# Output projection by seven products: other homes for the weight pieces, x added by accumulating transfers, another place for later loads

## The chip, the cores and the metric

The kernel runs on one core of a Trainium2 chip, in float32 accuracy throughout. The metric is the device time of one execution in microseconds (us), the median of the runs shown. A profile is one more execution, taken by the hardware profiler. In its rows PE is the matrix engine, PEld its weight loads, DVE, ACT and POOL the vector, scalar and GpSimd engines, SP the engine that issues most loads; SPq and POOLq are the queues of DMAs that SP and POOL issue. L955 is line 955 of the kernel.

## The reference

One decoder layer on x of 512 tokens by 1024 columns: a normalised input projection, two parallel token mixers, a gated merge, an output projection with a gated residual add, a second norm and a gated MLP of 2816 hidden columns.

```python
merged = (jax.nn.sigmoid(ga) * (out_a @ w_branch_swa[l])
          + jax.nn.sigmoid(gd) * (out_d @ w_branch_diff[l]))
x = x + gate1 * (merged @ w_out[l])

h2 = _rmsnorm(x, norm2_g[l]) * (1.0 + scale2) + shift2
x = x + gate2 * _conv_ffn(h2, w_up[l], conv_w[l], conv_b[l], w_down[l])
...
return _rmsnorm(x, final_g)
```

The change lies in `x + gate1 * (merged @ w_out)`, a product of 512x1024 by 1024x1024, and in what is loaded meanwhile for `h2 @ w_up`.

## The kernel before

**Seven products.** The output projection cuts merged and w_out (the gate is multiplied into its columns first) into two by two quarters and computes the product by seven quarter products in place of eight, named m1, m5, m6, p2, p3, m7, p4 in the order in which PE runs them (`mul_out`, L1178 is the matmul). Each has 512x512 weights, cut into two pieces p = 0, 1 of 256 rows, held as 128x1024 numbers. Every operand is split into a high part, rounded to the fast matmul format by a cast on ACT, and a low part, the rest, taken by a subtraction on DVE (`split`, L120); each product is then three matmuls: high by high, high by low, low by high. A product is 24 matmuls of 128x512, 12 for each piece.

**The chain of weights.** The weights of m1, m5 (called t1), m6 (t2) and p4 (t4) are running sums. Piece p of them lives in one buffer, `chain_o[p]` (chain_oy for p = 0, chain_ofgb for p = 1), which starts as a quarter of w_out. When the piece in it has been split, a DMA with accumulation, issued by POOL (`add_by_dma`, L955), adds the next term: first a quarter kept in DRAM scratch (b12g0, b12g1), then p3raw0 or p3raw1 (the piece of p3's weights), then p2raw0 or p2raw1. p3raw itself gets b12g added when p3's piece (b22) has been split, and then is the piece of m7 (t3). So each accumulating transfer waits for a split, and the cast of the next piece waits for the transfer.

**Homes.** A split piece (its two parts, whi and wlo) is kept either in a ring of three (`ring_home`, wp, WB = 3), where it waits for the piece three before to have been used, or in a buffer of its own, gT2 (`own_home`). Before the change the pieces m1p0, t2p0, b22p0 and t4p0 take gT2 in turn, the others the ring. The buffers vvh and vvl (`gpart(0)` and `gpart(1)`) hold xn0 and xn1 all the while; xn1 and the second half of the g1b tile keep three product sums (c1, c3, c2).

**Sums.** PE accumulates in three pairs of banks: oU (m1, then m6 and m7 on top, then p4), oV (m5, then p3), oX (p2). x1 is a tile of 512x1024 into which SP loads x in four transfers of 512 KB (L1150). Where a sum is wanted before its bank goes on accumulating, `keep_sum` has ACT copy the pair to c1, c2 or c3, and POOL accumulates that copy into x1 from SBUF. At the end DVE subtracts or adds the banks into x1 directly (`merge_x`, L1257), ACT squares (`square2`, L1266) for the second norm, and a few small DVE steps make its factor (L1275, L1283, L165 to L167). p4 goes on in bank oU only after DVE has subtracted m7's sum (x1 rows 256 to 511, second half of the columns).

**What follows.** xn rows are transposed on PE into th, ACT and DVE scale them (L1303, L1301) to bh and bl, and the up stage (`mul_slot`, L1202) runs in slots J. Its weights come by SP (`load_raw`, L990: wa for a11 and a12, s1, s3, a22), the s1 and s3 blocks with a second block that POOL accumulates (L992). wa1_0 and wa1_1 are split ahead of their slot into early_outh and early_outl (`hi_early`, `lo_early`, L1344, L1348).

**The order.** From `man` on, PE, DVE, ACT and POOL run in the order in which the code is written (manual schedule); SP's order was left to the scheduler. The transfers that POOL issues form one queue, as do SP's. A wait blocks what stands behind it on its engine.

Of the kernel before, what the change touches and what calls it, by code (L numbers as in the profile page):

```python
# [9 lines left out]
F32R = mybir.dt.float32r  # L10
# [37 lines left out]
def kernel(  # L48
# [896 lines left out]
    chain_o = [bp.tile([P, 2, S], F32, tag=g, name=f"chain_o{g}") for g in ("y", "fgb")]  # L945
    g4 = gpart(4, [P, 2, D], "g1b")
    g1b, c2 = g4[:, 0], g4[:, 1].rearrange("p (u n) -> p u n", u=2)
    st = gpart(3, [P, 2, 4, 256], "s1_t1")
# [5 lines left out]
    def add_by_dma(dst, src):  # L954
        nc.gpsimd.dma_start(dst, src, accum_op=ALU.add)  # L955
# [192 lines left out]

    for t in range(NT):
        nc.sync.dma_start(x1[:, t], xd[t * P : (t + 1) * P, :])  # L1150

# [174 lines left out]
    man = ExitStack()  # L1326
    man.enter_context(tc.manual_schedule(engines={nc.vector.engine, nc.scalar.engine, nc.tensor.engine, nc.gpsimd.engine}))
# [48 lines left out]
    keep_sum(c2, oU, 0, 1, -1.0)
    piece("p3", 1, braw["p3", 1], ring_home("b22p1"))
    add_by_dma(braw["p3", 1], scratch_o(1))
    split_quarter(opA[0][:, 2], opA[1][:, 2], q11)
# [6 lines left out]
    mul_out("p3")
    piece("m7", 0, braw["p3", 0], ring_home("t3p0"))
    for u in range(2):
        merge_x(u, 0, oX[u], ALU.subtract)
    piece("m7", 1, braw["p3", 1], ring_home("t3p1"))  # L1390
    hi_early(2)
    lo_early(2)
    mul_out("m7")
    square2(0, 0)
    square2(1, 0)
    piece("p4", 0, chain_o[0], own_home("t4p0"))
    norm_first(0, 0)
# [3 lines left out]
    norm_start(0, 1)  # L1401
    piece("p4", 1, chain_o[1], ring_home("t4p1"))
# [536 lines left out]
```

## Time and profile before

| | |
|---|---|
| median of 3 runs | 703.98 us (703.77 to 705.58) |
| profiled execution, its own time | 704.4 us |
| its span | 702.6 us |
| mean granted PE clock | 0.981 |
| matmuls | 3997 |
| products m1 to m7 of the projection, and what runs beside them, to p4's first matmul | 292.73 to 351.55 |
| p4 and the second norm, to the unbroken part of the up stage | 351.55 to 393.85 |

Columns of a timeline: start, duration, engine, line, operation, out<-in by the program's names without numbers (t1p is piece 0 or 1 of t1; chain_ofgb<-b12g is the accumulating DMA of b12g1), shapes, count, and in brackets the engine's idle time before it and what ended it. The start of a DMA row is its issue. A table of windows has one row for each stretch: length, busy time of each engine with its instructions, granted clock, busy share of the 16 DMA engines, GB/s. In a DMA view "DMA to landing" is the time from issue to the last byte; q0 software_dynamic is what POOL issues, q1 hardware_dynamic what SP issues.

### The profile page before, as it was taken

Reading aid. Unit: us, or ns where it says so; the run is one execution under the profiler, and the core shown is the slowest. Engines: PE = TensorE matmul, PEld = TensorE weight load, DVE = VectorE, ACT = ScalarE, POOL = GpSimd, SP = SyncE. Lnnn points to the kernel's source line nnn. Section 1 sums busy time; section 2 is a strip of 40 time slices with the busy share of each in tenths; the row PEclk is TensorE's granted clock in tenths of the full one; section 3 lists DMA queues with packets and bytes.
Section 4 is the critical chain, followed back from the end, with each engine's and each line's share of the span. In section 5 each row is a group of like instructions: output and inputs, shape, how many; then the busy total and the mean of one; then the engine's idle time right before and its main releaser. Section 6 shows DMA issues by size and latency. Waiting matters only on the chain.

```text
span 702.6 us, 10831 instructions
## 1 busy us (share of the span) xinstructions
PE 674.0 (96%) x3997; PEld 594.3 (85%) x3997; DVE 575.6 (82%) x1028; ACT 413.5 (59%) x722; POOL 101.1 (14%) x125
## 2 busy tenths in 40 slices
PE   9999999999999999978598999999999999999995
PEld 8888888888888888756388999999999999888884
DVE  6988986967876677756556999988899999979997
ACT  7668876565653233246458666555656667655665
POOL 2000000011321100125000111111101101640300
PEclk9999999999999999988889999999999999999999
DMA  9951323434448976479942697887998758998903
GB/s 352 408 210 61 117 64 115 154 114 143 160 126 287 306 244 210 91 221 237 201 110 40 184 225 180 222 201 227 234 238 195 191 175 234 182 206 229 164 1 120
DMA packets 77061, 129.65 MB, mean 185 GB/s; under 512 B 4496, under 2 KB 49712, under 8 KB 77008
## 3 DMA queue, kind: packets, MB, share of 16 engines
q1 hardware_dynamic: 54272, 95.04, 39.8%
q0 software_dynamic: 22448, 33.71, 27.5%
q8 instruction: 31, 0.51, 0.3%
q10 hardware_dynamic: 288, 0.21, 0.1%
q14 instruction: 22, 0.18, 0.1%
HBM read 122.11 MB, written 3.16 MB: 178 GB/s over the span
## 4 chain that ended last, share of the span: by engine, by line
PE 35%; issue 9%; DVE 3%; DMA 2%; POOL 1%; ACT 1%; POOLq 0%; SPq 0%; DVEq 0%; ACTq 0%
PE up L1202 28%; PE dc L1868 6%; DMA s_t<-in_w_up_dram 1%; PE oU L1178 1%; DMA s<-in_w_up_dram 1%; POOL b L1854 1%; DVE p2wl L120 0%; DVE p_wlo L1024 0%; ACT sqo L1266 0%; DVE p2a L120 0%; DVE chain_kvB L1728 0%; DVE chain_outl L1730 0%; POOL s L992 0%; DVE p3wl L120 0%; DVE t4p_wlo L120 0%
## 5 line engine op out<-in xcount | busy, mean ns | idle before, releaser
L1202 PE MATMUL up<-bh,p_whi 128*128 128x256 f32 x232 | 65.8, 283 | 1.2 <-ACT p_whi L1020 1.2
L1202 PE MATMUL up<-bh,p_wlo 128*128 128x256 f32 x232 | 65.8, 283 | 0.8 <-DVE p_wlo L1024 0.8
L1202 PE MATMUL up<-bl,p_whi 128*128 128x256 f32 x232 | 65.7, 283 | 0.0
L992 POOL DMA_DIRECT2D s<-in_w_up_dram x21 | 29.0, 1504 | 181.1 <-DMA s<-in_w_up_dram 76.7
L1202 PEld LDWEIGHTS up<-bh,p_whi 128*128 128x128 f32 x232 | 44.5, 192 | 1.4 <-ACT p_whi L1020 1.4
L1202 PEld LDWEIGHTS up<-bh,p_wlo 128*128 128x128 f32 x232 | 44.5, 192 | 1.0 <-DVE p_wlo L1024 1.0
L1202 PEld LDWEIGHTS up<-bl,p_whi 128*128 128x128 f32 x232 | 44.5, 192 | 0.0
L1020 ACT CAST m_whi<-s 128x1024 fp32r<-128x1024 f32 x31 | 32.5, 1047 | 18.8 <-DVE s L1014 10.9
L1024 DVE TENSOR_TENSOR m_wlo<-s,m_whi 128x1024 fp32r<-128x1024 f32 x31 | 37.8, 1219 | 1.3 <-ACT m_whi L1020 1.3
L1202 PE MATMUL up<-t_kvB,m_whi 128*128 128x256 f32 x176 | 32.5, 284 | 0.2 <-DVE t_kvB L1324 0.2
L1202 PE MATMUL up<-t_outl,p_whi 128*128 128x256 f32 x176 | 32.2, 283 | 0.5 <-DVE pairs L1242 0.5
L1202 PE MATMUL up<-t_outh,m_whi 128*128 128x256 f32 x176 | 32.2, 283 | 0.0
L798 DVE CUSTOM_DVE_ANT_0 ra<-ra,csb 128x1024 f32<-128x1024 f32 x24 | 29.0, 1220 | 0.8 <-DMA ra<-in_w_ada_t_dram 0.7
L1202 PE MATMUL up<-t_kvA,m_whi 128*128 128x256 f32 x160 | 29.3, 283 | 0.0
L1202 PEld LDWEIGHTS up<-t_kvB,m_whi 128*128 128x128 f32 x176 | 27.5, 192 | 0.7 <-DVE t_kvB L1324 0.4
L1202 PEld LDWEIGHTS up<-t_outl,p_whi 128*128 128x128 f32 x176 | 27.4, 192 | 0.7 <-issue 0.7
L1202 PEld LDWEIGHTS up<-t_outh,m_whi 128*128 128x128 f32 x176 | 27.4, 192 | 0.0
L1020 ACT CAST p_whi<-wa 128x1024 fp32r<-128x1024 f32 x18 | 18.8, 1044 | 14.0 <-PE up L1202 8.6
L708 ACT ACTIVATE sd<-sd,dmx 128x128 f32<-128x128 f32 (+3 forms) x32 | 17.7, 556 | 14.9 <-DVE dmx L693 14.8
L1024 DVE TENSOR_TENSOR p_wlo<-wa,p_whi 128x1024 fp32r<-128x1024 f32 x18 | 22.0, 1223 | 4.0 <-ACT p_whi L1020 2.7
L1202 PE MATMUL up<-t_outh,m_wlo 128*128 128x256 f32 x88 | 25.0, 284 | 0.3 <-DVE m_wlo L1024 0.3
L1202 PEld LDWEIGHTS up<-t_kvA,m_whi 128*128 128x128 f32 x160 | 24.9, 192 | 0.0
(669 smaller groups left out, 2268.2 us busy)
## 6 DMA issues: line engine op xcount, KB each, us to landing
ra<-in_w_ada_t_dram SPq DMA_DIRECT2D x24, 512.0 KB, 4.1
wa<-in_w_up_dram SPq DMA_DIRECT2D x22, 512.0 KB, 5.5
s<-in_w_up_dram SPq DMA_DIRECT2D x21, 512.0 KB, 5.6
s<-in_w_up_dram POOLq DMA_DIRECT2D x21, 512.0 KB, 8.0
adaw<-in_w_ada_t_dram SPq DMA_DIRECT2D x15, 512.0 KB, 10.2
a<-in_w_up_dram SPq DMA_DIRECT2D x11, 512.0 KB, 5.0
b<-in_w_down_dram SPq DMA_DIRECT2D x10, 512.0 KB, 5.0
w<-in_w_first_dram SPq DMA_DIRECT2D x8, 512.0 KB, 10.2
```

Of the source, the lines that this page charges most:

```text
L708: nc.scalar.activation(pm[m], pm[m], AF.Exp, bias=mx[:, m : m + 1], scale=-1.0, accum_out=(l0, l1)[m])
L798: nc.vector.tensor_tensor_reduce(r, r, csb, 1.0, 0.0, ALU.mult, ALU.add, late_mod[:, idx : idx + 1])
L992: nc.gpsimd.dma_start(dst, upblock(*blk), accum_op=ALU.add)
L1020: nc.scalar.copy(W[J, name][0], R[J, SRC[name]])
L1024: nc.vector.tensor_sub(lo, R[J, SRC[name]], hi.bitcast(F32))
L1178: nc.tensor.matmul(o[u], a(k, u), w[:, q], start=name in ("m1", "m5", "p2") and k == 0 and x == 0, stop=k == 3 and x == 2, skip_group_chec ...
L1202: nc.tensor.matmul(o[u], w[:, k, cu], b[:, k], start=name in ("p1", "m5", "p2") and k == 0 and x == 0, stop=k == 3 and x == 2, skip_group_ ...
L1854: nc.gpsimd.dma_start(w, wblock(g, *add), accum_op=ALU.add)
L1868: nc.tensor.matmul((bank2[u] if o is None else o)[:, sl], a[:, q, cu], b[:, q, sl], start=first_mm and x == 0, stop=last_mm and x == 2, sk ...
```

## The change

Four things change in the projection's stage; the seven products, their order on PE and the numbers of casts and subtractions stay.

1. **Homes.** m1p0 goes to the ring and t1p0 to gT2; t2p0 and t3p0 go to vvh, t2p1 and t3p1 to vvl, b22p0 to gT2, t4p0 and t4p1 to the ring. xn0 and xn1 are taken after that. The copies c1, c2 and c3 are gone, and the g1b tile is half as large.
2. **x1.** ACT writes the first sum straight into x1 (`start_x`), and POOL accumulates x from DRAM on top of it, for three of the four blocks; only the fourth (rows 256 to 511, first 512 columns) is loaded by SP.
3. **Order of splits.** p2p0's split, opB's split, p3's pieces, opA's third part and m7's and p4's pieces are written earlier; the splits of wa1_0 and wa1_1 later (the second behind p4's first matmuls), and so is the subtraction of oX.
4. **SP in written order**, with s3 and s1 and a22 of slots 0 and 1 written ahead of p4.

```diff
-    piece("m1", 0, chain_o[0], own_home("m1p0"))
+    piece("m1", 0, chain_o[0], ring_home("m1p0"))
...
-    piece("m5", 0, chain_o[0], ring_home("t1p0"))
+    piece("m5", 0, chain_o[0], own_home(2, "t1p0"))
...
-    for t in range(NT):
-        nc.sync.dma_start(x1[:, t], xd[t * P : (t + 1) * P, :])
+    xrows = [xd[2 * i * P : 2 * (i + 1) * P, :].rearrange("(t p) n -> p t n", p=P) for i in range(2)]
+    nc.sync.dma_start(x1[:, 2:4, :S], xrows[1][:, :, :S])
...
-    def keep_sum(dst, bank2, t, hf, sign):
+    def start_x(bank2, i, hf, sign):
+        sl = slice(hf * S, (hf + 1) * S)
         for u in range(2):
-            nc.scalar.activation(dst[:, u], bank2[u], AF.Copy, scale=sign)
-        add_by_dma(x1[:, t : t + 2, hf * S : (hf + 1) * S], dst)
+            nc.scalar.activation(x1[:, 2 * i + u, sl], bank2[u], AF.Copy, scale=sign)
+        add_by_dma(x1[:, 2 * i : 2 * i + 2, sl], xrows[i][:, :, sl])
...
-    piece("m6", 0, chain_o[0], own_home("t2p0"))
-    keep_sum(c1, oU, 0, 0, 1.0)
+    piece("m6", 0, chain_o[0], own_home(0, "t2p0"))
     add_by_dma(chain_o[0], braw["p2", 0])
+    V.tensor_add(q22, q22, q12)
+    piece("p2", 0, braw["p2", 0], ring_home("b21p0"))
+    start_x(oU, 0, 0, 1.0)
...
+    piece("p4", 0, chain_o[0], ring_home("t4p0"))
+    piece("p4", 1, chain_o[1], ring_home("t4p1"))
+    mul_out("m7")
+    xnp = [gpart(0, [P, 2, D], "xn0")]
+    square2(0, 0)
+    square2(1, 0)
     hi_early(1)
     lo_early(1)
...
+    load_s3(0)
+    load_s1(1)
+    load_a22(0)
+    load_s3(1)
+    load_a22(1)
     mul_out("p4", us=(0,))
```

POOL's transfers in the stage, before (x1 from xn1 and from g1b are the kept sums):

```order
L955 DMA chain_ofgb_2343<-b12g1_2351 128x2x512
L955 DMA chain_oy_2342<-b12g0_2350 128x2x512
L955 DMA chain_oy_2342<-p3raw0_2860 128x1024
L955 DMA chain_ofgb_2343<-p3raw1_2863 128x1024
L955 DMA x1_2873<-xn1_2841 128x2x512
L955 DMA chain_oy_2342<-p2raw0_2866 128x1024
L955 DMA chain_ofgb_2343<-p2raw1_2869 128x1024
L955 DMA x1_2873<-xn1_2841 128x2x512
L955 DMA p3raw0_2860<-b12g0_2350 128x2x512
L955 DMA x1_2873<-g1b_2344 128x2x512
L955 DMA p3raw1_2863<-b12g1_2351 128x2x512
```

and with the change:

```order
L954 DMA chain_oy_2342<-b12g0_2350 128x2x512
L954 DMA chain_ofgb_2343<-b12g1_2351 128x2x512
L954 DMA chain_oy_2342<-p3raw0_2858 128x1024
L954 DMA chain_ofgb_2343<-p3raw1_2861 128x1024
L954 DMA chain_oy_2342<-p2raw0_2864 128x1024
L954 DMA x1_2871<-in_x_dram 128x2x512
L954 DMA chain_ofgb_2343<-p2raw1_2867 128x1024
L954 DMA p3raw0_2858<-b12g0_2350 128x2x512
L954 DMA x1_2871<-in_x_dram 128x2x512
L954 DMA p3raw1_2861<-b12g1_2351 128x2x512
L954 DMA x1_2871<-in_x_dram 128x2x512
```

The first two change places; the accumulates into x1 come from DRAM and stand behind chain_oy<-p2raw0, p3raw0 and p3raw1.

SP's loads from x on, before (x4 is four transfers):

```order
L1150 DMA x1_2873<-in_x_dram 128x1024 x4
L990 DMA s3_0_3291<-in_w_up_dram 128x4x256
L990 DMA s1_1_3294<-in_w_up_dram 128x4x256
L990 DMA wa1_0_2972<-in_w_up_dram 128x4x256
L990 DMA wa1_1_2974<-in_w_up_dram 128x4x256
L990 DMA wa2_0_3694<-in_w_up_dram 128x4x256
L990 DMA wa2_1_3739<-in_w_up_dram 128x4x256
L990 DMA a22_0_3297<-in_w_up_dram 128x4x256
L990 DMA s3_1_3299<-in_w_up_dram 128x4x256
L990 DMA a22_1_3302<-in_w_up_dram 128x4x256
L990 DMA s1_2_3736<-in_w_up_dram 128x4x256
```

and with the change:

```order
L1147 DMA x1_2871<-in_x_dram 128x2x512
L989 DMA wa1_0_2966<-in_w_up_dram 128x4x256
L989 DMA wa1_1_2968<-in_w_up_dram 128x4x256
L989 DMA s3_0_3137<-in_w_up_dram 128x4x256
L989 DMA s1_1_3140<-in_w_up_dram 128x4x256
L989 DMA a22_0_3143<-in_w_up_dram 128x4x256
L989 DMA s3_1_3145<-in_w_up_dram 128x4x256
L989 DMA a22_1_3148<-in_w_up_dram 128x4x256
L989 DMA wa2_0_3689<-in_w_up_dram 128x4x256
L989 DMA s1_2_3731<-in_w_up_dram 128x4x256
L989 DMA wa2_1_3734<-in_w_up_dram 128x4x256
```

The loads s3_0 and s1_1, which stood ahead of wa1_0 and wa1_1, now stand behind them, and wa2_0 and wa2_1 behind a22_1 and s1_2.

DVE from the split of m7's second piece (t3p1) on, ahead of p4, before (the subtraction of oU0, which p4 waits for, follows three small steps after the last row):

```order
L120 TENSOR_TENSOR t3p1_wlo_3082<-p3raw1_2863,t3p1_whi_3081 128x1024
L1348 TENSOR_TENSOR early_outl_3048<-wa1_1_2974,early_outl_3048 128x1024
L120 TENSOR_TENSOR t4p0_3116<-chain_oy_2342,t4p0_3116 128x1024
L1271 TENSOR_SCALAR sso00_3111<-sso00_3111 128x2
L1257 TENSOR_TENSOR x1_2873<-x1_2873,oV0_2880 128x512
L1257 TENSOR_TENSOR x1_2873<-x1_2873,oV1_2881 128x512
L1275 SCALAR_TENSOR_TENSOR ms2_0_3127<-sso01_3121,sso00_3111 128x2
L120 TENSOR_TENSOR t4p1_wlo_3132<-chain_ofgb_2343,t4p1_whi_3131 128x1024
L1283 RECIPROCAL r02_0_3129<-r02_0_3129 128x2
```

and with the change:

```order
L120 TENSOR_TENSOR t3p1_3046<-p3raw1_2861,t3p1_3046 128x1024
L1254 TENSOR_TENSOR x1_2871<-x1_2871,oX0_2877 128x512
L1254 TENSOR_TENSOR x1_2871<-x1_2871,oX1_2878 128x512
L120 TENSOR_TENSOR t4p0_wlo_3076<-chain_oy_2342,t4p0_whi_3075 128x1024
L120 TENSOR_TENSOR t4p1_wlo_3080<-chain_ofgb_2343,t4p1_whi_3079 128x1024
L1350 TENSOR_TENSOR early_outh_3041<-wa1_0_2966,early_outh_3041 128x1024
L1268 TENSOR_SCALAR sso00_3108<-sso00_3108 128x2
L1254 TENSOR_TENSOR x1_2871<-x1_2871,oV0_2875 128x512
L1254 TENSOR_TENSOR x1_2871<-x1_2871,oV1_2876 128x512
L1272 SCALAR_TENSOR_TENSOR ms2_0_3123<-sso01_3117,sso00_3108 128x2
L1280 RECIPROCAL r02_0_3125<-r02_0_3125 128x2
```

The splits of t4p1 and early_outh and the subtraction of oX stand ahead of the norm's steps now, and the split of early_outl no longer stands in this row.

More of the change, by code (lines that the diff above doesn't have):

```diff
@@ L945 @@
     chain_o = [bp.tile([P, 2, S], F32, tag=g, name=f"chain_o{g}") for g in ("y", "fgb")]
-    g4 = gpart(4, [P, 2, D], "g1b")
-    g1b, c2 = g4[:, 0], g4[:, 1].rearrange("p (u n) -> p u n", u=2)
+    g1b = gpart(4, [P, D], "g1b")
     st = gpart(3, [P, 2, 4, 256], "s1_t1")
@@ L1113, in ring_home, with own_home @@
         return [wp.tile([P, 2, S], F32R, tag=g, bufs=WB, name=f"{name}_{g}") for g in ("whi", "wlo")]
-    def own_home(name):
-        t = gpart(2, [P, 2, 2, S], name, F32R)
+    def own_home(i, name):
+        t = gpart(i, [P, 2, 2, S], name, F32R)
         return [t[:, 0], t[:, 1]]
@@ L1326 @@
     man = ExitStack()
[L1327 removed]
+    man.enter_context(
+        tc.manual_schedule(
+            engines={nc.vector.engine, nc.scalar.engine, nc.tensor.engine, nc.gpsimd.engine, nc.sync.engine}
+        )
+    )
     V, q0, q1 = nc.vector, ks(0), ks(1)
[L1330 removed]
+    def start_x(bank2, i, hf, sign):
+        sl = slice(hf * S, (hf + 1) * S)
         for u in range(2):
[L1332 to L1333 removed]
+            nc.scalar.activation(x1[:, 2 * i + u, sl], bank2[u], AF.Copy, scale=sign)
+        add_by_dma(x1[:, 2 * i : 2 * i + 2, sl], xrows[i][:, :, sl])
     def split_quarter(hi, lo, src, qs=(slice(0, 4),), sign=1.0):
@@ L1356 @@
     split_quarter(opA[0][:, 1], opA[1][:, 1], q22, both, -1.0)
-    piece("m6", 0, chain_o[0], own_home("t2p0"))
-    keep_sum(c1, oU, 0, 0, 1.0)
+    piece("m6", 0, chain_o[0], own_home(0, "t2p0"))
     add_by_dma(chain_o[0], braw["p2", 0])
+    V.tensor_add(q22, q22, q12)
+    piece("p2", 0, braw["p2", 0], ring_home("b21p0"))
+    start_x(oU, 0, 0, 1.0)
     mul_out("m5")
-    piece("m6", 1, chain_o[1], ring_home("t2p1"))
+    piece("m6", 1, chain_o[1], own_home(1, "t2p1"))
     add_by_dma(chain_o[1], braw["p2", 1])
-    piece("p2", 0, braw["p2", 0], ring_home("b21p0"))
-    V.tensor_add(q22, q22, q12)
     piece("p2", 1, braw["p2", 1], ring_home("b21p1"))
@@ L1367 @@
     load_a(1, 1)
+    split_quarter(opB[0], opB[1], q22)
+    piece("p3", 0, braw["p3", 0], own_home(2, "b22p0"))
+    add_by_dma(braw["p3", 0], scratch_o(0))
     mul_out("m6")
-    keep_sum(c3, oV, 2, 1, -1.0)
-    split_quarter(opB[0], opB[1], q22)
+    start_x(oV, 1, 1, -1.0)
+    piece("p3", 1, braw["p3", 1], ring_home("b22p1"))
+    add_by_dma(braw["p3", 1], scratch_o(1))
     m5w = bp.tile([P, 2, 4, 256], F32R, tag="m5w", name="m5w")
     prep(0, "m5", (m5w[:, 0], m5w[:, 1]))
-    piece("p3", 0, braw["p3", 0], own_home("b22p0"))
-    add_by_dma(braw["p3", 0], scratch_o(0))
+    split_quarter(opA[0][:, 2], opA[1][:, 2], q11)
     mul_out("p2")
[L1376 to L1379, printed above, removed]
+    start_x(oU, 0, 1, -1.0)
     nc.gpsimd.dma_start(R[0, "s1"], upblock(0, 0, 0), accum_op=ALU.add)
@@ L1383 @@
         W[1, name] = early_w[2 + i][:, 0], early_w[2 + i][:, 1]
+    piece("m7", 0, braw["p3", 0], own_home(0, "t3p0"))
+    piece("m7", 1, braw["p3", 1], own_home(1, "t3p1"))
+    mul_out("p3")
+    for u in range(2):
+        merge_x(u, 0, oX[u], ALU.subtract)
+    piece("p4", 0, chain_o[0], ring_home("t4p0"))
[4 more added lines that the diff above has]
+    square2(1, 0)
     hi_early(1)
     lo_early(1)
[L1386 to L1396, printed above, removed]
     norm_first(0, 0)
@@ L1401 @@
     norm_start(0, 1)
-    piece("p4", 1, chain_o[1], ring_home("t4p1"))
     rs = norm_end(0)
@@ L1413 @@
     b11, b21 = (big.tile([P, 4, 256], F32, tag=f"h{g}B", name=f"braw{n}") for g, n in (("h", "11"), ("l", "21")))
+    hi_early(2)
+    lo_early(2)
+    xnp.append(gpart(1, [P, 2, D], "xn1"))
     early(0, "act")
```

7 lines of the change are left out of this document (removed).

## The prediction

> **What bounds the kernel now.** I read the page's busy shares first, then the table of windows for the stretches of the stage the diff touches, then the groups' idle times of PE behind it, then the timelines of PE, DVE, ACT and POOL from 280 to 360, and the DMA view last.
>
> ```profile
> PE 674.0 (96%) x3997; PEld 594.3 (85%) x3997; DVE 575.6 (82%) x1028; ACT 413.5 (59%) x722; POOL 101.1 (14%) x125
> core 0: us, PE busy (x) PEld busy (x) DVE busy (x) ACT busy (x) POOL busy (x), PEclk, DMA share, GB/s
> 292.73:351.55 58.82, 43.26 (x145) 31.71 (x144) 32.98 (x46) 28.66 (x42) 13.82 (x13) 0.83 0.94 205
> 351.55:393.85 42.30, 38.62 (x273) 35.51 (x273) 28.27 (x45) 28.14 (x53) 3.85 (x3) 0.96 0.35 81
> 393.85:590.00 196.15, 196.15 (x1634) 196.15 (x1635) 182.26 (x265) 116.99 (x174) 23.98 (x20) 1.00 0.83 212
> ```
>
> PE is busy 96% of the span, and between 393.85 and 590 all the time: an earlier start of that stretch goes to the end one for one. The room lies in the first window, products m1 to m7 of the output projection: 43.26 busy of 58.82, at a granted clock of 0.83 and a DMA share of 0.94. The changed code is nearly all there. Its end is the first matmul of p4, and the rows ahead of that, read upwards, name what was late.
>
> ```profile
> 327.87 2.14 POOL L955 DMA_DIRECT2D p3raw<-b12g  x1
> 339.54 1.04 ACT L120 CAST t3p_whi<-p3raw 128x1024 fp32r<-128x1024 f32 x1 [4.20 <-DMA p3raw<-b12g]
> 340.61 1.23 DVE L120 TENSOR_TENSOR t3p_wlo<-p3raw,t3p_whi 128x1024 fp32r<-128x1024 f32 x1 [2.82 <-ACT t3p_whi L120]
> 345.09 1.28 DVE L1257 TENSOR_TENSOR x<-x,oV 128x512 f32<-128x512 f32 x2
> 347.36 0.16 DVE L1275 SCALAR_TENSOR_TENSOR ms<-sso,sso 128x2 f32<-128x2 f32 x1 [0.99 <-ACT sqo L1266]
> 348.79 1.23 DVE L120 TENSOR_TENSOR t4p_wlo<-chain_ofgb,t4p_whi 128x1024 fp32r<-128x1024 f32 x1 [1.26 <-ACT t4p_whi L120]
> 349.93 0.16 DVE L1283 RECIPROCAL r<-r 128x2 f32<-128x2 f32 x1
> 350.72 1.29 DVE L1257 TENSOR_TENSOR x<-x,oU 128x512 f32<-128x512 f32 x2
> 351.55 1.19 PE L1178 MATMUL oU<-t4p,a2h 128*128 128x512 f32 x2 [5.42 <-DVE x L1257]
> ```
>
> p4 waits until DVE has taken m7's sum out of bank oU; DVE gets there after a norm and three splits; all of that starts with t3p1, whose input p3raw1 was ready only when an accumulating DMA issued at 327.87 had landed (cast at 339.54). So the stage is bound by a chain of accumulating DMAs: each waits for the split of the value that it overwrites, and the next piece waits for it. 339.54 to 351.55 is 12.0 us.
>
> **The change, part by part.** The product order on PE and the counts of splits stay; the four accumulates of xn and g1b into x1 become three of x from DRAM, and four 512 KB loads of x one.
>
> 1. The first chain (homes of m1p0 and t1p0). Rows of before:
>
> ```profile
> 283.59 1.24 POOL L955 DMA_DIRECT2D chain_ofgb<-b12g  x1 [17.07 <-DVE m1p_wlo L120]
> DMA to landing us min/median/max: 6.1/6.1/6.1
> 291.74 1.24 POOL L955 DMA_DIRECT2D chain_oy<-b12g  x1 [6.91 <-DVE m1p L120]
> 298.00 1.04 ACT L120 CAST t1p_whi<-chain_oy 128x1024 fp32r<-128x1024 f32 x1 [3.71 <-DMA chain_oy<-b12g]
> 295.05 0.43 DVE L1082 TENSOR_TENSOR merged_outl<-merged_outl,merged_outh 128x256 f32<-128x256 f32 x1
> 299.08 1.23 DVE L120 TENSOR_TENSOR t1p_wlo<-chain_oy,t1p_whi 128x1024 fp32r<-128x1024 f32 x1 [3.60 <-ACT t1p_whi L120]
> 300.82 0.68 DVE L1072 SCALAR_TENSOR_TENSOR merged_outl<-merged_outl,pB 128x512 f32<-128x512 f32 x1
> 305.95 1.23 DVE L120 TENSOR_TENSOR t1p_wlo<-chain_ofgb,t1p_whi 128x1024 fp32r<-128x1024 f32 x1 [0.25 <-ACT t1p_whi L120]
> 307.47 0.85 POOL L955 DMA_DIRECT2D chain_ofgb<-p3raw  x1 [5.99 <-DVE t1p_wlo L120]
> ```
>
> The second row is from the tile view of chain_ofgb around 283.59 (least, median, most). With m1p0 in the ring, POOL's slot at 283.59 goes to chain_oy and not the one at 291.74: it lands at 289.7 and no longer ends ACT's wait at 298.00. DVE idled 3.60 for that cast: its work ends at 295.48, one split is moved ahead of that point (spacing 1.13, so 296.6), a quarter of opA's low part (128x512 as L1072, 0.68 with its drain) is 0.6, and L1072 starts at 297.2, not 300.82. From L1072 to the split of t1p1 are 5.13: 302.3, not 305.95. The issue behind it comes 1.52 later (307.47 less 305.95): 303.8. The new wait (ACT's cast of t1p0 on the DMA) has a cast of a2h behind it, at most 1.04 as that cast, covered while DVE still works up to 295.5.
>
> 2. The second chain.
>
> ```profile
> chain_ofgb<-p3raw POOLq DMA_DIRECT2D x1, 512.0 KB, 9.3
> DMA to landing us min/median/max: 5.2/5.2/5.2
> 302.33 2.76 SPq L1150 DMA_DIRECT2D x<-in_x_dram  x4
> 316.84 1.04 ACT L120 CAST t2p_whi<-chain_ofgb 128x1024 fp32r<-128x1024 f32 x1 [7.96 <-DMA chain_ofgb<-p3raw]
> 317.92 1.23 DVE L120 TENSOR_TENSOR t2p_wlo<-chain_ofgb,t2p_whi 128x1024 fp32r<-128x1024 f32 x1 [8.40 <-ACT t2p_whi L120]
> 319.44 0.84 POOL L955 DMA_DIRECT2D chain_ofgb<-p2raw  x1 [8.00 <-DVE t2p_wlo L120]
> ```
>
> chain_ofgb<-p3raw took 9.3 with four loads of x issued ahead of it; its twin on chain_oy took 5.2 (second row, that tile's view). With one load of x I take 5.2: landing at 309.0, cast then, split 1.07 later (317.92 less 316.85) and next issue 1.52 after that: chain_ofgb<-p2raw1 at 311.6, not 319.44. DVE then has b21p1, the split of opB and b22p0, at 1.13 to 1.22 each: b22p0 at 313.5, so p3raw0<-b12g is issued at 315.0, and one split later p3raw1<-b12g at 316.4 (327.87).
>
> 3. The software queue. That is now earlier than POOL's DMAs can be served, so the queue sets p3raw1's landing.
>
> ```profile
> q0 software_dynamic: 1311, 2.00, 115.2%
> q1 hardware_dynamic: 11, 0.01, 0.3%
> q0 software_dynamic: 603, 1.75, 74.8%
> q1 hardware_dynamic: 1058, 1.05, 29.3%
> ```
>
> The first two rows are the DMA view from 331 to 341, the others from 311 to 323 (packets, MB, share). Alone, the queue moves 2.00 MB in 10 us: 0.2 MB per us, 2.62 for a piece of 0.524 MB. From 309.0 on stand in it, by the new order: chain_oy<-p2raw0, x into (0,0), chain_ofgb<-p2raw1, p3raw0, x into (1,1), p3raw1. Six times 2.62 is 15.7, to 324.7. Hardware loads beside it cost: in the second window 1.75 MB took 8.75 of the 12 us, so 1.05 MB of loads cost 3.25, 3.1 us per MB. wa1_0 is issued when chain_oy<-p2raw0 has landed (near 311.7): 0.524 MB, 1.6 us. wa1_1, s3_0 and s1_1 come when chain_ofgb<-p2raw1 has landed (309.0 + 3 x 2.62 + 1.6 = 318.5); beside the last three accumulates (1.57 MB) pass 0.6 byte for each of theirs (1.05 by 1.75): 0.94 MB, 2.9 us. p3raw1 lands at 324.7 + 1.6 + 2.9 = **329.2**; the cast was at 339.54.
>
> Bounds of that term: loads that cost nothing give 324.7; wa1_0 and three loads paid in full (4 x 1.6 = 6.4) 331.1. I take the middle case, since its window has both queues full as here. Two of the six, x from DRAM into x1, are an operation that no row shows. Nearest are b12g into p3raw (DRAM, accumulated), 2.62 by the window above, and the transfers into x (view of that tile: least, median, most from issue to landing), up to 11.0:
>
> ```profile
> DMA to landing us min/median/max: 5.1/7.5/11.0
> ```
>
> I take 2.62; twice that puts p3raw1 5.2 later.
>
> That packets of two queues take turns one for one is a rival: the window has 603 against 1058, so they did not there, but had they to, 1.57 MB (541 packets) would let 541 of some 1 KB pass, 0.54 MB, 1.7 us for 2.9, and the time would be 1.2 lower, 691.8. The Trainium skill, "DMA: Bandwidth & Descriptors", section "Queues, rings and completion order", says that each DMA engine goes round its queue rows and drains one packet before it switches; by that rule the loads put beside the accumulates hold them up packet by packet, and the sum would come out at 691.8. The trace does not agree in the count of packets (603 to 1058), so the sum stays with the bytes measured.
>
> 4. From p3raw1 to p4. Cast at 329.2, split of t3p1 at 330.27 (1.07). Now DVE has, at the same spacings: bank oX out of x 331.4 (the pair 1.2), splits of t4p0 332.6, t4p1 333.74 and early_outh 334.88, oV out of x 336.1. Then as before: 345.09 to ms 347.36 is 2.27, so ms at 338.37; the reciprocal no longer stands behind t4p1's split, so it follows ms by 0.5; 349.93 to 350.72 is 0.79: oU at 339.67, p4 0.83 later at **340.5**. That is 11.3 from landing where it was 12.0. Of the three edits, t4p1's split out of the norm gains, and early_outh and oX in DVE's row cost. Gain: 351.55 - 340.5 = 11.0.
>
> PE's own work must not be late. Its step, from two rows of p2:
>
> ```profile
> 328.62 0.39 PE L1178 MATMUL oX<-b21p_wlo,a2h 128*128 128x512 f32 x1
> 328.85 0.39 PE L1178 MATMUL oX<-b21p_whi,a2l 128*128 128x512 f32 x1
> ```
>
> From 311.3, when t2p1's split is done, there are 12 steps of m6, 24 of p2, 24 of p3 and 12 of m7: 72 at 0.23 end at 327.9. m7's last 12 begin when t3p1's split is done, 331.5, and end at 334.3, at half the clock at 337.0: ahead of oU's turn at 339.67.
>
> 5. Behind p4. early_outl's cast and split now stand on ACT and DVE ahead of the evacuation of th.
>
> ```profile
> 356.76 0.56 ACT L1303 ACTIVATE braw<-th,late_mod 128x256 f32<-128x256 f32 x1 [4.83 <-PE th L1293]
> DMA to landing us min/median/max: 3.4/6.5/17.2
> L990 SPq DMA_DIRECT2D s<-in_w_up_dram x5: 368/410/514, 305.2 to 392.7; - x5
> 412.55 1.06 ACT L1020 CAST p_whi<-wa 128x1024 fp32r<-128x1024 f32 x1
> ```
>
> ACT idles 4.83 there, so a cast of 1.06 is hidden if wa1_1 has landed. Its issue is at 318.5; the longest such load took 17.2 (second and third row: loads of L990 issued from 300 to 400), 335.7, ahead of p4. Without that cover each late us is paid. On SP, now in written order, wa1_1's wait has s3_0, s1_1, a22_0, s3_1, a22_1 behind it, and wa2_1 stands behind s1_2. The last load of s in that view was issued at 392.7; behind it, wa2_1 would land by 410.3 even with 17.2, before the cast at 412.55, where wa is next wanted. I cost these at nothing; a later one costs PE its lateness. The second window's idle time of PE, 3.7 us, shifts rigidly.
>
> **Sum.** 11.0 us from 704.4, the profiled execution (span 702.6), is 693.4. That execution is 0.4 above the median shown, 703.98, so the forecast for the median is **693.0**.
>
> **Rivals.**
> - Cheaper loads: nothing for them in step 3 moves p3raw1 to 324.7 and the time 4.5 lower, to 688.5. For it: the software queue was not full all through the window that I priced them by. Against it: in that window the accumulates moved 1.75 MB where 2.40 would have passed alone. Chance 0.20, with the 0.07 of turns one for one in it.
> - Dearer x: two accumulates at 5.2 each give 698.2. Against it: nothing in b12g's rows is dear, and that also reads DRAM. 0.10.
> - Slower: the same mechanism with more. The two accumulates of x stand in POOL's order ahead of p3raw1, so each microsecond of excess on one is paid twice; the gain of 11.0 is gone at an excess of 5.5 each. At a spacing of 11.0 (the longest landing above; excess 8.4, 16.8 in all) p3raw1 lands at 346.0 and the time is 709.8. Against it: accumulates overlap in the queue, 2.62 apart, so a landing time is not a spacing. 0.04.
> - The change doesn't bring chain_oy forward: if the split of m1p0, which the first slot now waits for, is not done before 290, chain_oy keeps the slot of 291.74, the chain keeps its times, and the median is 704.0. Against it: POOL's wait of 17.07 at 283.59 ends on DVE's split and not on data, and the order puts m1p0's there. Or the time comes back behind p4 through a load; against it ACT's 4.83 idle. 0.06.
>
> **How the numbers follow.** Forecast (692 to 695, all loads in full give 694.9) 0.55; cheaper loads 0.20; below 688.5, if the norm chain is shorter too, 0.05; dearer x 0.10; no change 0.06; slower 0.04. The range 688.5 to 698 leaves out 0.05, 0.06, 0.04 and a few hundredths of dearer x. A measurement of this kernel tells 0.3% (2.1 us) from no change. Faster by over that: 0.55 + 0.20 + 0.05 + 0.10 = 0.90; within it 0.06; slower 0.04.
>
> **What would show it.** Step 1: ACT's cast of t1p0 no longer waits near 298, and chain_ofgb<-p3raw is issued near 303.8. Step 2: it takes about 5 and not 9.3. Step 3: the cast of t3p1 at 329, accumulates of x 2.6 apart. Step 4: p4 begins near 340.5, with DVE's x L1254 as its releaser. Step 5: th's evacuation some 5 after p4, and no idle of PE in the up stage. A landing of p3raw1 after 334, or a wait for wa or s in the up stage, would make the prediction wrong.

## The result and the profile after

The changed kernel takes 693.3 us (median of 4 runs, 693.08 to 693.46), the kernel before 703.88 in the same comparison (4 runs, 702.73 to 705.58): ratio 0.9848, 95% interval 0.9827 to 0.9868, some 10.6 us. The forecast was 693.0, range 688.5 to 698. The profiled execution is 693.14, its span 691.4.

The busy shares and the windows of the same stages, cut at 340.00 (0.27 behind p4's first matmul) and at the start of the unbroken stretch:

```profile
PE 668.7 (97%) x3997; PEld 591.8 (86%) x3997; DVE 575.2 (83%) x1028; ACT 413.1 (60%) x722; POOL 100.6 (15%) x125
292.73:340.00 47.27, 37.72 (x146) 29.05 (x145) 32.03 (x47) 26.76 (x40) 13.58 (x12) 0.91 0.87 178
340.00:382.60 42.60, 39.24 (x274) 35.94 (x274) 29.50 (x47) 29.18 (x55) 3.85 (x3) 0.94 0.59 132
382.60:578.70 196.10, 196.10 (x1635) 196.06 (x1634) 181.97 (x264) 116.90 (x173) 24.20 (x20) 1.00 0.83 212
```

p4 begins at 339.73 where it began at 351.55, 11.8 earlier. From there to the unbroken stretch are 42.9 us (42.30 before), and that stretch is as long as before (196.10 and 196.15): nearly all that was won ahead of p4 went to the end. The matmul work in the first window is nearly the same number of instructions (145, 146) in 5.5 us less busy time, at a granted clock of 0.91 where it was 0.83.

The timeline of the changed kernel, POOL, ACT, DVE and PE rows in order of time, against the rows that the prediction shows of before:

```profile
283.92 1.24 POOL L954 DMA_DIRECT2D chain_oy<-b12g  x1 [17.66 <-DVE m1p_wlo L120]
289.98 1.05 ACT L120 CAST t1p<-chain_oy 128x1024 fp32r<-128x1024 f32 x1 [0.84 <-DMA chain_oy<-b12g]
297.43 0.68 DVE L1071 SCALAR_TENSOR_TENSOR merged_outl<-merged_outl,pB 128x512 f32<-128x512 f32 x1
302.55 1.23 DVE L120 TENSOR_TENSOR t1p_wlo<-chain_ofgb,t1p_whi 128x1024 fp32r<-128x1024 f32 x1 [0.25 <-ACT t1p_whi L120]
304.07 0.85 POOL L954 DMA_DIRECT2D chain_ofgb<-p3raw  x1 [10.03 <-DVE t1p_wlo L120]
308.67 1.05 ACT L120 CAST t2p<-chain_ofgb 128x1024 fp32r<-128x1024 f32 x1 [2.23 <-DMA chain_ofgb<-p3raw]
311.27 0.88 POOL L954 DMA_DIRECT2D chain_ofgb<-p2raw  x1 [2.77 <-DVE t2p L120]
314.68 1.21 POOL L954 DMA_DIRECT2D p3raw<-b12g  x1 [2.53 <-DVE b22p L120]
316.12 2.24 POOL L954 DMA_DIRECT2D p3raw<-b12g  x1
321.67 1.05 ACT L120 CAST t3p<-p3raw 128x1024 fp32r<-128x1024 f32 x1 [4.32 <-DMA p3raw<-b12g]
328.48 1.04 ACT L120 CAST t3p<-p3raw 128x1024 fp32r<-128x1024 f32 x1 [5.76 <-DMA p3raw<-b12g]
338.90 1.28 DVE L1254 TENSOR_TENSOR x<-x,oU 128x512 f32<-128x512 f32 x2
339.73 0.76 PE L1175 MATMUL oU<-t4p_whi,a2h 128*128 128x512 f32 x1 [4.51 <-DVE x L1254]
```

The same chain sets p4, about 12 us earlier. ACT's wait for the first accumulate is 0.84 where it was 3.71; POOL issues chain_ofgb<-p3raw at 304.07 (307.47), and the cast that waits for it comes 4.6 later and not 9.37; from that cast to the issue of p3raw0 are 6.0 and not 9.5.

The trace starts of two executions are not to be compared to the tenth: the first accumulate of the stage is issued at another time in each profile, whatever the change behind it.

```profile
281.96 1.24 POOL L954 DMA_DIRECT2D chain_oy<-b12g  x1 [16.86 <-DVE m1p_wlo L120]
285.94 1.24 POOL L954 DMA_DIRECT2D chain_oy<-b12g  x1 [18.71 <-DVE m1p_wlo L120]
```

These are the earliest and the latest of all profiles here (runs e12 and e4 below), and the two kernels do not differ ahead of them. So each stage is read as an interval within one trace. Six intervals make up the way from that first issue to p4's first matmul (us, from the POOL rows, the landings of the transfers and the PE row, here and below):

| | a | b | c | d | e | f | sum |
|---|---|---|---|---|---|---|---|
| before | 23.88 | 9.35 | 9.50 | 7.90 | 5.24 | 12.09 | 67.96 |
| after | 20.15 | 4.57 | 6.04 | 6.91 | 6.82 | 11.32 | 55.81 |
| difference | -3.73 | -4.78 | -3.46 | -0.99 | +1.58 | -0.77 | -12.15 |

a: first accumulate of b12g issued, to chain_ofgb<-p3raw1 issued. b: to its landing. c: to p3raw0<-b12g issued. d: to its landing. e: to the landing of p3raw1. f: to p4. The span fell by 11.2, since the stage began 0.33 later in this profile and the rest took 351.67, not 351.05; both differences are within the spread of the profiles here (the first issue comes at 281.96 to 285.94, and the rest takes 350.5 to 352.3).

### The profile page after: what moved, and what is told of

It reads as the page before. It is cut to its first block, busy times and chain, and to the rows that moved or that the text cites. A ratio compares the mean times of both kernels' runs of the same rounds, so it can differ in the third digit from the quotient of the medians.

```text
span 691.4 us, 10824 instructions
## 1 busy us (share of the span) xinstructions
PE 668.7 (97%) x3997; PEld 591.8 (86%) x3997; DVE 575.2 (83%) x1028; ACT 413.1 (60%) x722; POOL 100.6 (15%) x125
## 4 chain that ended last, share of the span: by engine, by line
PE 66%; issue 16%; DMA 10%; DVE 5%; POOL 1%; ACT 1%; POOLq 0%; SPq 0%; DVEq 0%; ACTq 0%
PE up L1199 28%; PE dc L1872 6%; PE av L374 3%; PE pga L123 2%; PE pga L124 2%; PE pga L125 2%; DMA p3raw<-b12g 2%; DMA wgd<-in_w_tiles_dram 2%; PE aqa L371 2%; PE sd L682 1%; PE sw L584 1%; DMA w<-in_w_first_dram 1%; PE pk L123 1%; PE pq L125 1%; PE pk L125 1%
## 5 line engine op out<-in xcount | busy, mean ns | idle before, releaser
L991 POOL DMA_DIRECT2D s<-in_w_up_dram x21 | 27.0, 1292 | 179.8 <-DVE a L1241 61.8
```

Of the source, the lines that this page charges most:

```text
L991: nc.gpsimd.dma_start(dst, upblock(*blk), accum_op=ALU.add)
```

## The experiments

**e1 and e2: the two large parts alone.** e1 is the kernel before with the homes of m1p0 and t1p0 exchanged:

```diff
-    piece("m1", 0, chain_o[0], own_home("m1p0"))
+    piece("m1", 0, chain_o[0], ring_home("m1p0"))
...
-    piece("m5", 0, chain_o[0], ring_home("t1p0"))
+    piece("m5", 0, chain_o[0], own_home("t1p0"))
...
-    piece("m6", 0, chain_o[0], own_home("t2p0"))
+    piece("m6", 0, chain_o[0], own_home("t2p0", 0))
```

> The kernel before with one part of the change alone: m1p0 to the ring, t1p0 to gT2, t2p0 to vvh (xn0 taken later). Theory A (a chain of accumulates, then POOL's queue): chain_ofgb<-p3raw1 is issued near 303.8 instead of 307.5, its landing still has the four x loads beside it and so takes some 9.3, 313.1; everything behind it 3.7 earlier, p3raw1 near 335.8, time near 700.3. Theory B (nearly all of the gain comes from taking the x loads away): the earlier issue only meets the loads, lands near 316.8 as before, time 703 to 704. Theory C (the two parts need each other not at all, and this is the larger): p3raw1 near 332, time 696 to 697.

e2 is the kernel before with `start_x` in place of `keep_sum`, at the same places, and one load of x:

```diff
-    keep_sum(c1, oU, 0, 0, 1.0)
+    start_x(oU, 0, 0, 1.0)
...
-    for t in range(NT):
-        nc.sync.dma_start(x1[:, t], xd[t * P : (t + 1) * P, :])
+    nc.sync.dma_start(x1[:, 2:4, :S], xrows[1][:, :, :S])
```

> The kernel before with the other part alone: the first sums written into x1 by ACT, x added by POOL from DRAM at the places of the old kept sums, one SP load of x in place of four. Theory A: chain_ofgb<-p3raw1 is issued at 307.5 as before but takes 5.2 and not 9.3, landing at 312.7; everything behind 4.1 earlier, time near 699.8. Theory B: 693 to 695. Theory C: the landing is no better (POOL's own queue, not the loads, made it 9.3), time 703 to 704.

e1: 700.43 beside 704.86, ratio 0.9938 (0.9915 to 0.996). e2: 702.27 beside the same, 0.9961 (0.9945 to 0.9976). The view of chain_ofgb's transfer (least, median, most from issue to landing; first e1, then e2):

```profile
DMA to landing us min/median/max: 8.4/8.4/8.4
```

```profile
DMA to landing us min/median/max: 5.8/5.8/5.8
```

Theory A holds for both: the homes give interval a (20.30 in e1) and leave b long (8.4), the x part gives b (5.79 in e2) and leaves a (23.90). e2's median is 2.5 above A's 699.8. Its intervals sum to 64.10, 3.9 less than before, with b at 5.8 and not 5.2; in its profile the stage begins 1.0 later than in that of before, and the kernel before took 704.86 in this comparison. Together the gains of 4.4 and 2.6 make 7.0, and the change gave 10.6.

**e10: both parts together,** without the new order of splits and of SP's loads.

> The kernel before with the two single parts together (homes of m1p0, t1p0 and t2p0; x begun by ACT and added by POOL, one SP load), without the new order of splits and of SP. Theory D: the two add, 4.4 + 2.6, or a little more as the earlier issue no longer meets the four loads: time 696 to 698, p3raw0 issued some 9.5 behind the landing of chain_ofgb<-p3raw1. Theory A: the whole gain but for the 0.8 behind p3raw1: near 694.2.

697.53 beside 704.63, ratio 0.9892 (0.9861 to 0.9923). a is 20.15 and b 4.58, as in the changed kernel: with both, the one x load is done before the accumulate is issued. What is missing against the changed kernel are 3.9 us (sum of the intervals 59.69), and they lie in c, 9.56 (6.04 there), and f, 12.06 (11.32); d and e together are 0.4 shorter.

```profile
303.94 0.85 POOL L955 DMA_DIRECT2D chain_ofgb<-p3raw  x1 [10.04 <-DVE t1p_wlo L120]
318.08 1.22 POOL L955 DMA_DIRECT2D p3raw<-b12g  x1 [4.06 <-DVE b22p L120]
```

p3raw0 is issued 14.1 behind chain_ofgb<-p3raw1; in the changed kernel it was 10.6 (304.07 to 314.68). Theory A as on record (the queue alone) is out by 3.3, theory D is borne out.

**e9: the order of splits undone alone,** in the changed kernel.

```diff
-    V.tensor_add(q22, q22, q12)
-    piece("p2", 0, braw["p2", 0], ring_home("b21p0"))
     start_x(oU, 0, 0, 1.0)
...
+    piece("p2", 0, braw["p2", 0], ring_home("b21p0"))
+    V.tensor_add(q22, q22, q12)
     piece("p2", 1, braw["p2", 1], ring_home("b21p1"))
...
+    prep(0, "m5", (m5w[:, 0], m5w[:, 1]))
     piece("p3", 0, braw["p3", 0], own_home(2, "b22p0"))
```

> The changed kernel with DVE's and ACT's row of splits behind t2p1 as it was before the change (b21p0, the sum for opB and the split for m5w ahead of b22p0), POOL's order as changed. p3raw0<-b12g is issued some 3.4 later behind the landing of chain_ofgb<-p3raw1 (three DVE steps of 1.13). Theory D (the part that the two single parts lacked, 3.7 us, is this order of splits: p3raw0's issue must come before POOL's queue runs empty): p3raw0 is issued about when chain_ofgb<-p2raw1 lands, the queue runs empty, p3raw1 lands 2 to 3.5 later, time 695.5 to 697. Theory A as I had it (from chain_ofgb<-p3raw1 on, the queue alone sets p3raw1, whatever the splits do): 693.3, at most 0.5 more.

698.05 beside 704.63, ratio 0.9898 (0.9871 to 0.9926): 4.75 above the changed kernel's median (4.0 with each set against the kernel before beside it), where theory D expected 2.2 to 3.7. c is 9.52 (3.5 more), and d 8.97 (2.1 more). The DMA view of e9 from 317.1 to 322.8 (packets, MB, share), and the view of wa there and in the changed kernel:

```profile
q1 hardware_dynamic: 1209, 1.19, 72.5%
q0 software_dynamic: 36, 0.07, 11.1%
DMA to landing us min/median/max: 4.0/4.0/4.0
```

```profile
DMA to landing us min/median/max: 14.1/14.1/14.1
```

chain_ofgb<-p2raw1 lands at 317.10 in e9 and releases wa1_1, s3_0 and s1_1 on SP, issued at 317.17, 317.59 and 318.18; p3raw0 is issued among them, at 317.34, and in these 5.7 us 1.19 MB of loads pass and next to nothing of the accumulates. wa1_1 lands in 4.0. In the changed kernel p3raw0 was issued 3.3 ahead of wa1_1, which took 14.1 while the accumulates went on. Not all of e9's empty time is due to the loads: in the changed kernel too POOL's queue moves next to nothing just ahead of p3raw0's data, as its DMA view from 317.2 to 318.0 shows:

```profile
q1 hardware_dynamic: 270, 0.28, 98.4%
q0 software_dynamic: 11, 0.00, 0.8%
```

There the data of p3raw0 begin at 318.2, 3.5 behind its issue at 314.68; in e9 they begin at 322.0, 4.7 behind. The load that passes in this view, wa1_0, is no more than a small part of the 3.5: with no load beside it (e12 below) p3raw0 lands only 0.65 sooner behind its issue. So the order of splits is worth 3.5 for DVE's three steps (c) and some 1.4 for who comes first (d is 2.1 longer, e 0.7 shorter; 60.68 less 55.81 is 4.9).

**e5: the SP part undone,** loads where the scheduler had put them.

```diff
-            engines={nc.vector.engine, nc.scalar.engine, nc.tensor.engine, nc.gpsimd.engine, nc.sync.engine}
+            engines={nc.vector.engine, nc.scalar.engine, nc.tensor.engine, nc.gpsimd.engine}
...
-    load_s3(0)
-    load_s1(1)
...
```

> The changed kernel with its SP part undone: SP's order left to the scheduler, the loads of s3, s1 and a22 at their old place, so s3_0 and s1_1 stand ahead of wa1_0 again. Theory A (each load beside an accumulate costs it time, wherever it is put): s3_0 and s1_1 now go beside chain_ofgb<-p3raw1 (4.6 to about 5.8 us, as with x alone changed) and no longer beside the last three accumulates (10.4 to about 9.5): p3raw1 within 0.5 of 328.4, time near 693.5. Rival (the SP order is what the two single parts lack: they gave 4.4 and 2.6, the whole 10.6): time near 697.

693.31 beside 704.59, ratio 0.9849 (0.9823 to 0.9876), the changed kernel's. Theory A is right in the time and its reason half right: b is 4.60, not 5.8 (s3_0 and s1_1 were issued 4.7 and 4.2 ahead of the accumulate and had mostly passed), and e is 6.69: loads of wa ran beside the accumulates in place of those of s. The order of SP is no part of the gain.

**e6: the loads held back** until t3p1's cast.

```diff
-    load_a(1, 1)
...
+    nc.sync.dma_start(gate_row, pieces["m7", 1][0][0:1, 0].bitcast(F32))
+    load_a(1, 1)
```

> The changed kernel with the loads of wa1_1, s3_0 and s1_1 held back on SP until the cast of t3p1 (by a store of one row of its result into scratch, on which the loads wait in SP's order): they no longer run beside the last three accumulates. Theory A (loads cost by their bytes): the three accumulates take 3 x 2.62 = 7.9 and not 10.45 from the landing of chain_ofgb<-p2raw1; p3raw1 near 325.8, p4 near 337.1, time near 690.7, if wa1_1 still lands ahead of its cast. Theory of one-for-one turns, as I sized it: 1.7 earlier, near 691.6. Rival (loads cost nothing): p3raw1 stays at 328.4, time 693.3.

691.2 beside 704.59, ratio 0.981 (0.9785 to 0.9836). e falls from 6.82 to 5.11, two accumulates of 2.56, so the loads cost 0.85 beside each of these; but d rises from 6.91 to 7.77, which no theory here expected. So from p3raw0's issue to p4 0.85 is gained of the 2.6 that the byte estimate gave. The median is 2.1 lower all the same, near theory A's 690.7, but the profile does not lay that to the loads: its stage begins 0.82 earlier and the rest takes 0.56 less, as varies from profile to profile. Why p3raw0 lands later where wa1_1, s3_0 and s1_1 are held back stays open; e8 has it too (7.38), and in e3, e5, e7 and e11 d is 6.8 to 7.2.

**e3 and e4: x behind p3raw1.** e3 moves one accumulate of x behind p3raw1 (and behind the other half's), e4 both that stood ahead. The edit of e3, the helper `add_x` left out; e4 treats `start_x(oU, 0, 0, 1.0)` in the same way:

```diff
-    start_x(oV, 1, 1, -1.0)
+    start_x(oV, 1, 1, -1.0, add=False)
...
     start_x(oU, 0, 1, -1.0)
+    add_x(1, 1)
```

> The changed kernel with one accumulate of x, the one into rows 256 to 511, second half, issued behind p3raw1's and behind that of the other half instead of ahead of p3raw1's. Theory A (POOL's queue, first in first out at 2.62 us each, sets p3raw1's landing): p3raw1 lands 2.6 earlier (328.4 to 325.8), p4 begins near 337.1, time near 690.7. Rival (splits or PE set it, and the queue only looks full): p3raw1 and the time do not move, 693.3.

> The changed kernel with both accumulates of x that stand ahead of p3raw1's issued behind it. Theory A: two places of 2.62 less: p3raw1 lands near 323, p4 begins near 334, time near 688; below that the issue of p3raw1 (316.1) and PE's own work (m7 not before about 333) become the bound. Rival (only one place can be gained, since chain_ofgb<-p2raw1 is issued no earlier than 311.3 and sets p3raw0 and p3raw1 behind it): near 690.7 as with one accumulate moved. Rival (queue not the bound): 693.3.

e3: 689.41 beside 704.86, ratio 0.9781 (0.9759 to 0.9804). ACT's casts of t3p0 and t3p1 in e3:

```profile
321.62 1.05 ACT L120 CAST t3p<-p3raw 128x1024 fp32r<-128x1024 f32 x1 [4.51 <-DMA p3raw<-b12g]
324.98 1.05 ACT L120 CAST t3p<-p3raw 128x1024 fp32r<-128x1024 f32 x1 [2.31 <-DMA p3raw<-b12g]
```

They are 3.36 apart, not 6.81: the accumulate of x between them had cost 3.45, as much as one of b12g beside the same loads. So x from DRAM is not dearer, and behind p3raw0 the queue does set the landing.

e4: 691.53 (689.16 to 693.71) beside 704.86, ratio 0.98 (0.9768 to 0.9832). Its profile is of the slowest of four executions, 693.71, with the late start of its stage quoted above. Its intervals say why the second place gives nothing: d is 6.93, as in the changed kernel (6.91), for p3raw0 is not waiting for the queue but lands some 7 behind its own issue; e is 2.81 (3.36 in e3); and f is 12.79, since DVE now waits for x:

```profile
330.64 1.28 DVE L1254 TENSOR_TENSOR x<-x,oX 128x512 f32<-128x512 f32 x2 [1.36 <-DMA x<-in_x_dram]
```

The second rival on record (one place only can be gained) came true.

**e7: oU subtracted ahead of the norm.**

```diff
-    norm_start(0, 1)
-    rs = norm_end(0)
     merge_x(2, 1, oU[0], ALU.subtract)
     merge_x(3, 1, oU[1], ALU.subtract)
+    norm_start(0, 1)
+    rs = norm_end(0)
```

> The changed kernel with the subtraction of oU (which p4 waits for) written ahead of the norm's small steps. Theory A (p4's start is the end of the stage, set by DVE's row of work behind p3raw1): oU follows oV at 336.6, p4 at 337.4 instead of 339.7; the norm is done 0.2 to 1.2 later, ahead of the transposes; time near 691.0. Rival (the norm sets the end and not p4, the transposes wait for xn instead): 693.3.

691.03 beside 704.59, ratio 0.9804 (0.9778 to 0.983). In e7's DVE rows oU follows oV, and the norm's first step comes right behind:

```profile
334.72 1.27 DVE L1254 TENSOR_TENSOR x<-x,oV 128x512 f32<-128x512 f32 x2
335.91 1.27 DVE L1254 TENSOR_TENSOR x<-x,oU 128x512 f32<-128x512 f32 x2
337.11 0.15 DVE L1272 SCALAR_TENSOR_TENSOR ms<-sso,sso 128x2 f32<-128x2 f32 x1
```

f is 8.98 instead of 11.32. DVE would have idled there for ACT's squares in any case, and the transposes of xn, which begin 4.4 behind p4, had room.

**e8, e11 and e12: versions from these.** e8 has the edits of e3, e6 and e7, e11 those of e3 and e7, e12 those of e8 with wa1_0 held back until t3p0's cast as well.

> The changed kernel with three edits of the runs here together: the accumulate into x (rows 256 to 511, second half) behind p3raw1's, the loads of wa1_1, s3_0 and s1_1 held back until the cast of t3p1, and oU subtracted ahead of the norm's steps. Theory A, the three terms add: p3raw1 near 323.2 (two accumulates of 2.62 behind 317.9), p4 near 332, 693.3 - 3.9 - 1.7 - 2.3 = 685.4. Rival (what is freed is taken up by PE's own work on p2, p3 and m7, or by the loads landing late): 687 to 689.

> The kernel of all three edits without the held-back loads: the accumulate into x behind p3raw1's and oU subtracted ahead of the norm's steps. If the loads cost what the run with them held back shows (some 0.9 on p4's start): 687.5. If holding them back only trades their cost for a late wa1_1: 686.6, as with it.

> The kernel of all three edits with the load of wa1_0 held back too, until the cast of t3p0 (again by a store of one row on which it waits), so that no load runs beside chain_ofgb<-p2raw1 and p3raw0. Theory A (a load costs the accumulate beside it; alone they follow each other at 2.56): chain_ofgb<-p2raw1 lands some 1.0 earlier, p3raw0 and p3raw1 each 2.56 behind, p3raw1 near 322.0 where all three edits had 324.4, time near 684.4, if wa1_0 still lands ahead of its cast (4.5 behind p3raw1). Rival (wa1_0 then comes with too little time: issued near 321, beside two accumulates, landing 328 or later, and the row of splits on DVE waits for it): 686 to 688. Rival (the gap of 4.1 to 4.5 ahead of p3raw0 is not wa1_0's): p3raw1 near 324, time 686.7.

| | time | before beside it | ratio (95%) | d | e | f |
|---|---|---|---|---|---|---|
| e8 | 686.65 | 704.59 | 0.9741 (0.9718 to 0.9763) | 7.38 | 2.56 | 9.00 |
| e11 | 687.69 | 704.63 | 0.9751 (0.9726 to 0.9777) | 6.81 | 3.74 | 8.99 |
| e12 | 690.45 | 705.05 | 0.9799 (0.9782 to 0.9817) | 6.26 | 2.55 | 13.62 |

e8 is below both kernels, 1.2 above theory A's sum, as the held loads brought 0.6 (e11 to e8, sum of d, e and f) where 1.7 had been put in. Whether e8 is better than e11 their intervals don't tell. e12 answers both of its questions: with no load beside it p3raw0 still takes 6.26, so the gap ahead of its landing is for the most part its own and not wa1_0's; and wa1_0 came too late:

```profile
331.21 1.04 ACT L1351 CAST early_outh<-wa 128x1024 fp32r<-128x1024 f32 x1 [4.62 <-DMA wa<-in_w_up_dram]
```

The split of early_outh stands on DVE ahead of oV and oU, so p4 paid for it: f is 13.62. That is the first rival's mechanism. The profiled execution took 687.85, within its 686 to 688; the other four took 690.34 to 691.25, and no profile shows why.

## Why the prediction was right, and where not

**Steps 1 and 2** came out within 0.4 us: the fourth merge step (L1072 before, L1071 now) 297.43 (297.2 forecast), t1p1's split 302.55 (302.3), issue 304.07 (303.8), landing 308.64 (309.0), chain_ofgb<-p2raw1 311.27 (311.6), p3raw0 314.68 (315.0), p3raw1 316.12 (316.4). As intervals, which the later start of the stage does not touch, a is 20.15 (20.2 forecast), b 4.57 (5.2) and c 6.04 (6.0). e1, e2 and e10 show that each part does what its step says.

**Step 3** ended at 328.41 where 329.2 was forecast, and that was luck: the parts of its sum were wrong. The step that failed is "the queue sets p3raw1's landing", with six places of 2.62 and 4.5 us for loads. The runs show in its place: with the new order p3raw0 lands 6.3 to 7.8 behind its own issue, POOL's queue moves next to nothing just ahead of its data (the view from 317.2 to 318.0 above), and its issue is set by DVE's row of splits (c; e9 and e10 lose 3.5 there, e4 gains nothing by a place ahead of it). Only the accumulates behind it wait for the queue, at 2.56 alone (e6) and some 3.4 beside loads (e3; 2.81 in e4, 3.74 in e11). 314.68 + 6.91 + 2 x 3.41 is 328.4. The six places came near since 15.7 + 4.5 is about 6.04 + 6.91 + 6.82 = 19.8. The earlier issue of p3raw0 was worked out in step 2 and then not used as a term; it is worth 3.5 of the 10.6.

**The term for loads** was mis-sized. Two accumulates beside them took 6.82 and alone 5.11: 1.7, by 0.36 MB of loads that passed meanwhile (DMA view of the changed kernel, 321.6 to 328.4):

```profile
q0 software_dynamic: 572, 1.11, 91.4%
q1 hardware_dynamic: 351, 0.36, 19.1%
```

Forecast were 2.9 for three accumulates, with 0.6 byte of load for each byte accumulated. That came from the prediction's window from 311 to 323 before the change, in which loads ran alone at first. Its parts, from 311 to 313.5 and from 313.5 to 319, and then e9 from 324 to 329:

```profile
q1 hardware_dynamic: 584, 0.58, 73.1%
q0 software_dynamic: 18, 0.07, 14.7%
q0 software_dynamic: 344, 0.90, 84.6%
q1 hardware_dynamic: 346, 0.35, 23.2%
q0 software_dynamic: 389, 0.76, 81.9%
q1 hardware_dynamic: 390, 0.40, 29.0%
```

Where both queues have work throughout, packets go one for one: 344 to 346, and 389 to 390. So the rival of turns had the mechanism right, and the prediction's reading of 603 against 1058 was wrong. The Trainium skill, "DMA: Bandwidth & Descriptors", section "Queues, rings and completion order", has each DMA engine go round its queue rows a packet at a time; the trace agrees, by these counts. The size that the prediction gave to the rival was off too: in e9 a packet of the accumulates is of some 2 KB and one of the loads of 1 KB, half a byte for each byte, and at 0.76 MB in 5 us an accumulate of 0.524 MB takes 3.45, near the 3.4 measured in e3 and in the changed kernel. The changed kernel's counts are unequal, 572 to 351, because its loads come in late: from 319.2 to 323 pass 390 packets of POOL's queue and 1 of SP's, though wa1_1 was issued at 318.02.

```profile
q0 software_dynamic: 390, 0.77, 112.3%
q1 hardware_dynamic: 1, 0.00, 0.1%
```

Turns alone do not explain that delay of some 5 us, and it stays open. wa1_0, 1.6 us in the sum, cost p3raw0 some 0.6 to 1.1 (d is 6.26 in e12, 6.81 in e11 and 7.38 in e8).

**Step 4** gave 11.3 from landing to p4, measured 11.32, in the order of DVE's steps that it listed. What its three edits of DVE's row (t4p1's split, early_outh, oX) come to together is shown by e9 and e10, which have the new row and the old and differ in f by 0.73 (11.33 and 12.06); they were not tried one by one.

**Step 5**: in the unbroken stretch PE's only wait (us in all, times, longest) is the one that it has before the change too, and it is not for a load:

```profile
PE up L1199 <- DVE pairs L1239: 0.5, 1, 0.5
```

and th's evacuation, at 345.55, stands 5.8 behind p4's start (5.2 before); e5 shows that the place of SP's loads cost nothing and gave nothing.

**Rivals.** Dearer x is refuted by e3 (3.45 for one of x). The slower case needed an excess of 5.5 on each and had none. Cheaper loads were partly true (1.7 for 2.9), and turns one for one are what the counts show. m1p0's split was done when the first slot needed it (POOL at 283.92, 283.59 before).

## What to carry to other kernels

Where accumulating transfers and splits alternate, ask of each transfer whether it waits for its own issue or for its queue: moving a split ahead helped the first kind (3.5 us here), moving another transfer behind helped the second (3.45), and moving a transfer out of the way of the first kind gave nothing (e4). Issue what is urgent before the event that releases bulk loads, since in e9 the loads released just ahead of it passed first. An operand that a later step needs only at its end (x here) belongs behind the transfers of the chain, up to the point where its own reader would wait.

## What had not been expected of the hardware

Loads released 0.2 ahead of an accumulate held it for 2 us or more, while accumulates queued ahead of the same load, the first by 3.3, made that load take 14.1 instead of 4.0. The times from issue to landing of the two accumulates into p3raw (least, median, most; the least is p3raw0), in e9, in the changed kernel and in e12 with no load beside them:

```profile
DMA to landing us min/median/max: 9.0/11.3/13.5
DMA to landing us min/median/max: 6.9/9.6/12.3
DMA to landing us min/median/max: 6.3/6.9/7.5
```

Before the change and in e1, e2 and e10, where wa1_1 is issued 0.5 to 1.4 ahead of it, p3raw0 takes 7.7 to 8.2.

p4's first matmuls, in turn, ran at a granted clock of 0.52 after PE's wait of 4.51, and later ones at 1.00:

```profile
339.70:345.00 5.30, 5.27 (x13) 4.11 (x14) 2.38 (x3) 1.44 (x2) 0.06 (x1) 0.52 1.16 182
345.00:356.00 11.00, 10.34 (x77) 9.57 (x75) 7.20 (x18) 7.78 (x18) 1.29 (x1) 1.00 0.71 201
```

In e7 PE waits 2.24 at that place, and the same 5.30 us ran at 0.68:

```profile
336.73 0.61 PE L1175 MATMUL oU<-t4p_whi,a2h 128*128 128x512 f32 x1 [2.24 <-DVE x L1254]
336.70:342.00 5.30, 5.27 (x21) 4.30 (x21) 3.18 (x8) 2.76 (x6) 2.71 (x2) 0.68 0.75 105
```

The Trainium skill, "TensorE: Matmul & The Clock Gate", Part 1, gives about 3.4 us of idleness ahead of the half clock and about 3.4 us of work ahead of the full one, counted in windows that run free of the kernel, so that the number of slow steps varies. The 4.51 agree with the first; 5.2 us of slow steps (339.73 to the transposes at 344.91) are longer than the second, and in e7 a wait of 2.24, behind the shorter waits of m7, was followed by slow steps too. Nor does the wait's length tell that of the slow stretch: e4 and e12 wait 7.03 and 6.97 at this place, and twelve and six slow steps follow; in e11 (3.74) six fast steps come ahead of six slow ones. The length of the wait was not varied by itself.
